# The first feed-forward of a fused block in six rounds of 4, 4, 4, 4, 4, 2 tiles in place of five of 6, 4, 4, 4, 4

## The chip, the cores and the metric

One core of one Trainium2 chip runs the kernel. The metric is device time in microseconds (us), the median of three runs. All times in the rows are microseconds from the start of one profiled execution.

## The reference, cut to what matters

The reference runs two layers of a mixed attention block, then a second block: a feed-forward with SwiGLU, a mixer of sparse and stick-breaking attention, a cross-attention to a memory of 256 tokens, and another feed-forward. There are 512 tokens (528 with the meta tokens of the first block) of width 1024; the inner width of the feed-forwards is 2816. What the change touches is this:

```
def swiglu(h, wg, wu, wd):
    return (jax.nn.silu(h @ wg) * (h @ wu)) @ wd
...
x = x + 0.5 * swiglu(rms_norm(x, ffn1_norm), ffn1_wg, ffn1_wu, ffn1_wd)
...
k = rms_norm((mem_n @ wk).reshape(B, M, MEM_HEADS, HEAD_DIM), g_k)     # in memory_cross_attention
v = (mem_n @ wv).reshape(B, M, MEM_HEADS, HEAD_DIM)
```

The memory's `k` and `v` depend on the input `mem` alone, so the kernel is free to place them early; it does so inside the first feed-forward.

## The kernel before

**Numbers.** Activations lie transposed, features on the 128 partitions and tokens along the free axis. Every fp32 operand of a large product is split into a high part (rounded to fp32r, by ScalarE) and a low part (the rest, by VectorE), and a product is three matmuls: high·high, high·low, low·high. `Stream` loads the weights in one fixed order (`weight_plan`) through SyncE's queue, and makes `whi` (line 135, ScalarE) and `wlo` (line 136, VectorE), each in three buffers, two entries ahead of use (`AHEAD = 2`).

**The feed-forward (`ffn`).** The inner width is 22 tiles of 128. They come in rounds (`ROUNDS`); `ffn_order` writes out the order. Within a round each tile is made by an "up" step, and after the round its tiles are multiplied by the down weights: eight `down` steps (one for each 128 of the 1024 outputs), each with 3 matmuls of 512 columns per tile of the round, and each ended by an addition into the residual `h` on VectorE (line 1266).

- Round 0 is *plain* (`up`): gate and up products over 8 blocks of the width, 2 × 8 × 3 = 48 matmuls of 512 columns per tile, then a scaling by the norm's factor, tanh, and products on VectorE.
- The later rounds are *blocks* (`up_blocks`): a 2×2 block scheme with seven products in place of eight, 7 × 4 × 3 = 84 matmuls of 256 columns per tile. It needs sums of weight blocks (`Stream.sums`, lines 156 to 159 and 164, 165, on VectorE and ScalarE), sums of activation blocks, and sums of the results (line 1188).
- Between the two stands *prepare*: it spreads the norm's factor (`Rn`), scales the residual (line 1160, 8 instructions), forms the activation sums `ta`, `tb` (lines 1167 to 1170) and splits them and the blocks `x0` to `x7` (lines 422 and 423). In the second feed-forward most of this is done earlier, during its plain tiles; in the first, where the memory's tensors occupy the space until their products are done, all of it comes after round 0.
- After prepare, `BEFORE[f]` of round 0's downs are emitted ahead of the first block tile; what is left of a round's downs is spread over the block tiles of the next round, and the last round's eight come at the end, each followed by the next norm's split and sum of squares (`norm_feed`).

The memory's products (`memory_kv`: first `k`, with a head norm on VectorE and a transpose, then `v`; 48 matmuls of 256 columns each) are put behind the plain tiles whose numbers `MEM_AT` gives.

**Order.** The kernel emits its instructions in this order, with some work put by an event queue that runs on an estimated clock (`at`, `soon`, `poll`); the framework (`schedule_with_timeline_sim=True`) then fixes one order per engine, by emission order and by the priorities raised with `high_priority`. Engines work in that order and wait for each other by semaphores. Three PSUM buffers (`mm`) take the plain and down products, two (`s`) share the block products.

Of the kernel before, what the change touches and what calls it, by code (L numbers as in the profile page):

```python
# [55 lines left out]
COLS = {"dq": 0, "dk": 512, "dv": 1024, "dg": 1536, "fq": 2048, "fk": 2560, "fv": 3072, "fg": 3592}  # L56
GA0 = (0, 2, 2, 0, 2, 0, 1, 1)
GA1 = (1, 1, 2, 0, 2, 0, 0, 2)
MEM_AT = (3, 5)

ROUNDS = {"ffn1": (6, 4, 4, 4, 4), "ffn2": (4, 4, 4, 4, 4, 2)}
EARLY, BLOCK_AHEAD = (7000.0, 11000.0), 3
BEFORE = {"ffn1": 8, "ffn2": 6}
ACTS = 8

S_LATE = 7
# [115 lines left out]
def ffn_order(f):  # L182


    out, m, down = [], 0, []
    for r, n in enumerate(ROUNDS[f]):
        for i in range(n):
            out.append(("blocks" if r else "plain", r, m + i, i))
            if f == "ffn1" and r == 0 and m + i in MEM_AT:
                out.append(("mem", r, m + i, i))  # L190
# [5 lines left out]
        if r == 0:  # L196
            out += [("prepare", r, 0, 0)] + down[:BEFORE[f]]
            down = down[BEFORE[f]:]
        m += n
# [3 lines left out]
def weight_plan(A):  # L203
# [16 lines left out]
    def halves(key, src, cols):  # L220
        for k in range(2):
            cut(key + (k,), src, cols, (512 * k, 512 * k + 512))

    def ffn(f):
        wg, wu, wd = (A[f"{f}_{x}_2"][0] for x in ("wg", "wu", "wd"))
        for kind, r, m, at in ffn_order(f):
# [6 lines left out]
            elif kind == "mem":  # L233
                x = "kv"[MEM_AT.index(m)]
                halves(("mem", x), A[f"mem_w{x}_2"][0], (0, 256))
# [61 lines left out]
class Net:  # L297
# [821 lines left out]
    def ffn(self, f, P, nxt, memory=None):  # L1119
# [4 lines left out]
        HT = T // 2  # L1124
        rounds = ROUNDS[f]
        with ExitStack() as st:
# [102 lines left out]
            for kind, r, m, at in ffn_order(f):  # L1229
# [11 lines left out]
                elif kind == "mem":  # L1241
                    mem("kv"[MEM_AT.index(m)])
                elif kind == "blocks":
# [870 lines left out]
```

## Time and profile before

| | us |
|---|---|
| median of 3 runs | 1791.04 (1790.66 to 1793.39) |
| the profiled execution: its own time | 1787.97 |
| the profiled execution: span from first to last instruction | 1786.2 |
| first feed-forward, first plain matmul to first matmul of the mixer | 672.1 to 1041.5 |
| second feed-forward | from about 1428 to the end |

PE is TensorE's matmuls, DVE VectorE, ACT ScalarE. A busy PE is one that always has a matmul under way. The granted clock (PEclk) is the share of full speed that TensorE was given; it has two levels, 1.2 and 2.4 GHz, and 1.00 is the higher. Matmul rows overlap: the pace is read from one start to the next.

### The profile page before, as it was taken

To read this page: it belongs to the slowest core of one execution; us is meant where nothing else is said; L and a number is where in the kernel's file an instruction comes from. 1 tells how busy PE (TensorE), PEld (TensorE's weight loads), DVE (VectorE), ACT (ScalarE), POOL (GpSimd) and SP (SyncE) were. 2 spreads that over 40 slices of the span, in tenths; PEclk is the share of its full clock that TensorE was granted. 3 is DMA by queue.
4 is the path that set the end of the run, shared out by engine and by line. 5 is a ranking of instruction groups with operands and counts; after the bars stand their busy time and mean duration, and the time that the engine had idled before them with its cause. 6 is when DMAs were issued, how large, how long until landed. Compare 5 with 4: busy or idle time off the path is not lost.

```text
span 1786.2 us, 31132 instructions
## 1 busy us (share of the span) xinstructions
PE 1723.6 (96%) x11949; PEld 1535.7 (86%) x11949; DVE 1384.1 (77%) x3305; ACT 940.9 (53%) x2051; POOL 33.6 (2%) x76
## 2 busy tenths in 40 slices
PE   7999999999999899999999999999978898999999
PEld 6999997998999678889999889877756787999997
DVE  6878666579876666699888778778787869988876
ACT  4656677356667863344433443457755634444432
POOL 1000000100000000000000000000000000000000
PEclk9999999999999999999999999999989999999999
DMA  4222211322222132332333243320101022333333
GB/s 159 74 69 72 67 54 37 95 60 83 70 74 60 37 120 83 109 128 83 101 105 109 70 142 129 91 71 14 37 24 48 31 76 95 96 100 102 100 91 104
DMA packets 56156, 146.00 MB, mean 82 GB/s; under 512 B 9032, under 2 KB 16840, under 8 KB 56008
## 3 DMA queue, kind: packets, MB, share of 16 engines
q1 hardware_dynamic: 54984, 143.95, 26.3%
q8 instruction: 94, 1.54, 0.3%
q14 instruction: 54, 0.44, 0.1%
q0 software_dynamic: 1024, 0.07, 0.1%
HBM read 141.83 MB, written 2.10 MB: 81 GB/s over the span
## 4 chain that ended last, share of the span: by engine, by line
PE 89%; DVE 6%; ACT 3%; issue 1%; DMA 1%; SPq 0%; ACTq 0%; DVEq 0%
PE mm L368 61%; PE s L368 18%; PE po L368 5%; PE pt L381 4%; PE pt L368 1%; DVE P L467 1%; DVE sc L1712 0%; DVE wlo L136 0%; ACT P L804 0%; ACT whi L135 0%; DMA w<-in_c_stream_dram 0%; DVE sbs L455 0%; ACT P L929 0%; DVE P L1714 0%; ACT PT L1616 0%
## 5 line engine op out<-in xcount | busy, mean ns | idle before, releaser
L135 ACT ACTIVATE whi<-w 128x1024 fp32r<-128x1024 f32 (+4 forms) x225 | 199.2, 886 | 267.0 <-PE mm L368 155.0
L136 DVE TENSOR_TENSOR wlo<-w,whi 128x1024 fp32r<-128x1024 f32 (+4 forms) x225 | 226.2, 1006 | 64.0 <-ACT whi L135 63.3
L368 PE MATMUL mm<-acth,whi 128*128 128x512 f32 x352 | 139.2, 397 | 3.5 <-DVE e L1143 1.7
L368 PE MATMUL mm<-actl,whi 128*128 128x512 f32 x352 | 139.7, 397 | 0.8 <-DVE actl L423 0.8
L368 PE MATMUL mm<-acth,wlo 128*128 128x512 f32 x352 | 139.3, 396 | 0.0
L381 PE MATMUL pt<-ident,P 128*128 128x128 f32 (+2 forms) x588 | 101.1, 282 | 17.6 <-DVE P L1714 11.7
L467 DVE CUSTOM_DVE_ANT_0 P<-s,mz 128x144 f32<-128x144 f32 (+8 forms) x195 | 82.8, 438 | 28.2 <-PE s L368 16.0
L381 PEld LDWEIGHTS pt<-ident,P 128*128 128x128 f32 (+2 forms) x588 | 65.2, 134 | 35.3 <-issue 15.7
L368 PE MATMUL mm<-cl,whi 128*128 128x264 f32 (+1 forms) x256 | 87.9, 344 | 0.5 <-DVE cl L1626 0.5
L368 PE MATMUL mm<-ch,wlo 128*128 128x264 f32 (+1 forms) x256 | 86.9, 341 | 0.5 <-DVE wlo L136 0.5
L368 PE MATMUL mm<-ch,whi 128*128 128x264 f32 (+1 forms) x256 | 84.7, 347 | 2.3 <-ACT ch L1008 1.4
L368 PEld LDWEIGHTS mm<-acth,whi 128*128 128x128 f32 x352 | 66.2, 188 | 19.3 <-DVE e L1143 2.1
L368 PEld LDWEIGHTS mm<-acth,wlo 128*128 128x128 f32 x352 | 66.3, 188 | 16.2 <-DVE wlo L136 0.2
L368 PEld LDWEIGHTS mm<-actl,whi 128*128 128x128 f32 x352 | 66.3, 188 | 15.8 <-DVE actl L423 1.3
L804 ACT ACTIVATE P<-P,nm 128x144 f32<-128x144 f32 (+4 forms) x136 | 68.0, 500 | 22.2 <-DVE nm L467 21.1
L1266 DVE SCALAR_TENSOR_TENSOR h<-mm,h 128x512 f32<-128x512 f32 x88 | 59.9, 682 | 9.7 <-PE mm L368 9.3
L164 ACT ACTIVATE whi<-sc 128x1024 fp32r<-128x1024 f32 x34 | 36.0, 1058 | 42.0 <-DVE sc L158 41.9
L368 PEld LDWEIGHTS mm<-ch,whi 128*128 128x128 f32 x256 | 47.2, 188 | 10.0 <-ACT ch L1008 2.3
L368 PE MATMUL s<-pk,pq 128*128 128x264 f32 (+4 forms) x171 | 54.4, 324 | 1.2 <-DVE nm L467 1.0
L368 PE MATMUL mm<-x0h,whi 128*128 128x264 f32 (+2 forms) x168 | 53.2, 317 | 1.5 <-DVE e L1143 0.6
L368 PE MATMUL mm<-x0h,wlo 128*128 128x264 f32 (+2 forms) x168 | 53.1, 316 | 0.9 <-DVE wlo L165 0.9
L368 PEld LDWEIGHTS mm<-ch,wlo 128*128 128x128 f32 x256 | 48.2, 188 | 6.4 <-DVE wlo L136 0.9
(840 smaller groups left out, 6032.8 us busy)
## 6 DMA issues: line engine op xcount, KB each, us to landing
w<-in_c_stream_dram SPq DMA_DIRECT2D x168, 512.0 KB, 3.6
w<-in_c_stream_dram SPq DMA_DIRECT2D x72, 256.0 KB, 2.6
w32b<-in_c_stream_dram SPq DMA_DIRECT2D x34, 512.0 KB, 3.6
w<-in_c_stream_dram SPq DMA_DIRECT2D x8, 384.0 KB, 3.1
h<-in_c_x_dram SPq DMA_DIRECT2D x8, 264.0 KB, 5.6
w1k<-in_cmp_w_k_dram SPq DMA_DIRECT2D x4, 512.0 KB, 5.4
w1v<-in_cmp_w_v_dram SPq DMA_DIRECT2D x4, 512.0 KB, 6.6
out_dram<-h SPq DMA_DIRECT2D x8, 256.0 KB, 2.0
```

Of the source, the lines that this page charges most:

```text
L135: nc.scalar.activation(out=hi, in_=w, func=AF.Copy)
L136: nc.vector.tensor_tensor(out=lo, in0=w, in1=hi.bitcast(F32), op=ALU.subtract)
L164: nc.scalar.activation(out=hi[:, :n], in_=src, func=AF.Copy)
L368: self.nc.tensor.matmul(out, lhsT, rhs, start=start, stop=stop)
L381: self.nc.tensor.transpose(out, in_, self.ident[:p, :p])
L467: self.nc.vector.tensor_tensor_reduce(out=dst, in0=s, in1=m, scale=-1.0, scalar=3.0e38, op0=ALU.add, op1=ALU.min, accum_out=nm)
L804: nc.scalar.activation(out=P_[:nq, a:b], in_=S[c][0], func=AF.Exp, bias=nm[:nq, 0:1], scale=S[c][1], accum_out=ls[:nq, c:c + 1])
L1266: v.scalar_tensor_tensor(out=H[m], in0=ps, scalar=0.25, in1=H[m], op0=ALU.mult, op1=ALU.add)
```

## The change

Three constants change: the first feed-forward's rounds, the plain tiles behind which the memory's products stand, and the number of round 0's downs that are emitted before the first block tile.

```diff
-MEM_AT = (3, 5)
-
-ROUNDS = {"ffn1": (6, 4, 4, 4, 4), "ffn2": (4, 4, 4, 4, 4, 2)}
+MEM_AT = (1, 3)
+
+ROUNDS = {"ffn1": (4, 4, 4, 4, 4, 2), "ffn2": (4, 4, 4, 4, 4, 2)}
 EARLY, BLOCK_AHEAD = (7000.0, 11000.0), 3
-BEFORE = {"ffn1": 8, "ffn2": 6}
+BEFORE = {"ffn1": 6, "ffn2": 6}
```

So two of the 22 tiles go from plain to blocks, there are six sets of eight downs in place of five (four tiles deep, the last two deep, where the first was six deep), `k` comes after plain tile 1 and `v` after plain tile 3, and two of round 0's downs go behind the first two block tiles. The order in which the weights are streamed follows.

## Rows read from the trace of the kernel before

**Rows 1.** The page's part 1: busy us, share, instructions.
```profile
PE 1723.6 (96%) x11949; PEld 1535.7 (86%) x11949; DVE 1384.1 (77%) x3305; ACT 940.9 (53%) x2051; POOL 33.6 (2%) x76
```
**Rows 2.** Timeline of PE: start, duration; pace of plain, memory and block tiles.
```profile
721.73 0.28 PE L368 MATMUL mm<-whi,x0h 128*128 128x256 f32 x1
...
727.33 0.39 PE L368 MATMUL mm<-x0h,whi 128*128 128x512 f32 x1
...
741.55 0.48 PE L368 MATMUL mm<-x4h,whi 128*128 128x512 f32 x1
...
749.93 0.28 PE L368 MATMUL mm<-whi,x0h 128*128 128x256 f32 x1
...
863.12 0.28 PE L368 MATMUL mm<-x0h,whi 128*128 128x256 f32 x1
...
873.12 0.40 PE L368 MATMUL mm<-acth,whi 128*128 128x512 f32 x1
```
**Rows 3.** Windows, first feed-forward: length, busy PE, PEld, DVE, ACT, POOL; PEclk, DMA.
```profile
756.50:790.20 33.70, 33.70 (x146) 27.09 (x146) 32.27 (x58) 15.30 (x26) 0.00 (x0) 1.00 0.39 129
756.50:773.35 16.85, 16.85 (x74) 13.54 (x74) 16.38 (x30) 8.38 (x16) 0.00 (x0) 1.00 0.45 156
857.50:873.12 15.62, 15.62 (x111) 14.52 (x109) 14.11 (x22) 6.35 (x9) 0.00 (x0) 1.00 0.39 119
1023.70:1045.80 22.10, 22.10 (x96) 17.78 (x95) 20.66 (x32) 15.69 (x24) 0.00 (x0) 1.00 0.50 144
```
**Rows 4.** Timeline of DVE: prepare's first instruction, the first block tile's last weight split.
```profile
757.85 0.74 DVE L1160 SCALAR_TENSOR_TENSOR yh<-h,gains,th 128x512 f32<-128x512 f32 x1
...
794.97 0.68 DVE L165 TENSOR_TENSOR wlo<-w32b,whi 128x512 fp32r<-128x512 f32 x1
```
**Rows 5.** Timeline of PE with the idle time before each: waits in both feed-forwards.
```profile
814.14 0.39 PE L368 MATMUL mm<-x0h,wlo 128*128 128x256 f32 x1 [0.69 <-DVE wlo L165]
...
824.54 0.39 PE L368 MATMUL mm<-x0h,whi 128*128 128x256 f32 x1 [0.32 <-ACT whi L164]
...
1476.98 0.50 PE L368 MATMUL mm<-acth,whi 128*128 128x512 f32 x1 [1.68 <-DVE e L1143]
...
1498.60 0.39 PE L368 MATMUL mm<-acth,whi 128*128 128x512 f32 x1
```
**Rows 6.** Groups of DVE by line and shape, 756.5 to 795.7: busy, mean ns.
```profile
L136 DVE TENSOR_TENSOR wlo<-w,whi 128x768 fp32r<-128x768 f32 x6 | 5.7, 947 | 0.8 <-ACT whi L135 0.8
L1266 DVE SCALAR_TENSOR_TENSOR h<-mm,h 128x512 f32<-128x512 f32 x8 | 5.4, 680 | 1.1 <-PE mm L368 1.1
...
L423 DVE TENSOR_TENSOR x2l<-yh,x2h 128x256 fp32r<-128x256 f32 x1 | 0.4, 415 | 0.0
```
**Rows 7.** The same groups of DVE, 850 to 912.4: four block tiles.
```profile
L136 DVE TENSOR_TENSOR wlo<-w,whi 128x512 fp32r<-128x512 f32 x8 | 5.5, 682 | 0.0
```
**Rows 8.** Windows of the second feed-forward: plain tiles 2 and 3, then downs.
```profile
1459.00:1473.00 14.00, 14.00 (x62) 11.43 (x61) 13.86 (x27) 6.97 (x13) 0.00 (x0) 1.00 0.20 57
1473.00:1495.40 22.40, 18.04 (x74) 13.25 (x73) 22.36 (x43) 10.55 (x18) 0.00 (x0) 1.00 0.20 59
```
**Rows 9.** Timeline of PE, ACT and DVE at the first feed-forward's plain tile 2.
```profile
699.62 0.39 PE L368 MATMUL mm<-x0h,whi 128*128 128x512 f32 x1
...
699.91 1.05 ACT L135 ACTIVATE whi<-w 128x1024 fp32r<-128x1024 f32 x1
700.42 2.73 DVE L668 SCALAR_TENSOR_TENSOR h<-h,gains,R 128x512 f32<-128x512 f32 x4
...
703.67 2.73 DVE L668 SCALAR_TENSOR_TENSOR h<-h,gains,R 128x512 f32<-128x512 f32 x4
...
706.92 1.22 DVE L136 TENSOR_TENSOR wlo<-w,whi 128x1024 fp32r<-128x1024 f32 x1
```
**Rows 10.** Timeline of PE in the memory stage: its longest wait there.
```profile
1398.09 0.58 PE L368 MATMUL s<-mk,mq 128*128 128x256 f32 x1 [4.63 <-ACT Pm L1981]
```
**Rows 11.** Window of the memory stage after that wait.
```profile
1398.00:1404.00 6.00, 5.91 (x31) 5.25 (x32) 5.69 (x21) 5.32 (x21) 0.00 (x0) 0.53 0.00 0
```

## The prediction

> **What bounds the kernel now.** I read the page first: PE is busy for 96% of the span [rows 1], so at first sight fewer matmuls mean less time. Then I followed the first feed-forward on PE's timeline, to see whether it paces the stage: from 672.1 to 1041.5 it waits twice, for 0.69 and 0.32 us, both times for the split of block weights by VectorE and ScalarE [rows 5]. So PE sets the pace, but VectorE is close behind. The windows show where: in the 33.70 us in which PE works off round 0's eight downs, VectorE is busy for 32.27 [rows 3]. It does prepare there, from 757.85 on, and ends the splits for the first block tile at 794.97 + 0.68 = 795.65 [rows 4], after PE has started that tile at 790.2. Round 0's downs, six tiles deep, are thus the cover for prepare, and a cover just long enough. Later there is more room: a block tile with two downs takes PE 15.62 us and VectorE 14.11 [rows 3].
>
> The second feed-forward already has the rounds that the first is to get. There VectorE is busy for 13.86 of 14.00 us and 22.36 of 22.40, and in the latter stretch PE works for 18.04 only [rows 8].
>
> **The change part by part.** The sum is made on the profiled execution's own 1787.97 us, which lies 3.07 below the median of the runs shown, 1791.04; I carry it over to the median. Less than 0.2% (3.6 us) can't be told from no change.
>
> *Two tiles from plain to blocks.* 36 plain matmuls take 749.93 − 741.55 = 8.38 us, 0.2328 each, so a plain tile's 48 take 11.17. A block tile's 84 take 873.12 − 863.12 = 10.00 [rows 2]. Twice the difference is **−2.3 us**. The down matmuls stay 22 × 3 × 8 = 528, and the memory's products stay as many as they are.
>
> *Eight more downs' endings and other weight loads.* Eight more additions into the residual cost VectorE 8 × 0.68 us [rows 6], and a block tile wants more of it than a plain one. In the rounds after the first block round this lies in the room of 15.62 − 14.11 = 1.5 us per tile [rows 3], and less is asked there of weights; I take nothing, and 1 us as the other bound. The stream's bytes are the same; the DMA engines are at 0.39 in the later block rounds [rows 3], so eight more loads cost nothing.
>
> *Prepare loses its cover.* It stands after `v` as before and can't start earlier: `Rn` is spread by PE only when `v`'s matmuls are issued, and the sums' space is the memory's. What VectorE has to do from there to the first block tile is 32.27 us less what shrinks: six weight splits of 768 columns at 0.95 become 512 wide at 0.68, −1.6 [rows 6, 7]; two downs, if they stay behind the block tiles, take with them 2 × 0.68 of addition and 2 × 0.68 of split, −2.7. That leaves 28.0 us. PE's cover is six downs of 12 matmuls, 16.85 us (a stretch of that length is in [rows 3]). The shortage is 11.1 us. If the framework brings the two downs forward, as it does in the second feed-forward, where down matmuls stand between a block tile's at 1498.60 [rows 5], the cover is 16.85 × 8/6 = 22.5, the work 30.7, and the shortage 8.2. If they stay, the two block tiles behind which they stand give some of the 11.1 back. The second feed-forward checks this from another side: its PE loses 22.40 − 18.04 = 4.4 us, though some 7.3 us of prepare are done there while plain tiles still run (of the 27 instructions 11 are for plain tiles and weights, and 13.86 − 11 × 0.6 is 7.3 [rows 8]), and six such instructions, 3.6 us, are left over into the downs. Without that lead, and with `v` as cover for the leftovers, 4.4 + 7.3 − 3.6 = 8.1. I take **+8.5 us**, with 4.4 and 11.1 as bounds. Behind VectorE, what stands still is PE alone; ScalarE is at 15.30 of 33.70 [rows 3].
>
> *The memory's `k` before plain tile 2.* Now tile 2 starts at 699.62 and its weights were ready before [rows 9]. With `k`'s weights ahead of them in the stream, two places of three buffers are taken, and tile 2's gate weights get the place that tile 3's have now: `whi` at 699.91, `wlo` at 706.92, because VectorE works off eight residual scalings first (line 668, 700.42 to 706.4), which were emitted earlier [rows 9]. `k` takes PE 727.33 − 721.73 = 5.6 us [rows 2], so tile 2 wants `wlo` with its third matmul, at about 699.6 + 5.6 + 0.5 = 705.7, and has it at 706.92 + 1.22 = 708.1. I take **+2.4 us**; bounds 0 (the framework puts this split ahead of the residual scalings) and 3.6 (it comes after one more instruction of its length). `k`'s head norm on VectorE comes in the plain tiles, where VectorE has room; the memory's split inputs are made while the layer before still runs, so they are not late. Queued behind the waiting matmul is all of PE; nothing else is near its limit there.
>
> *The last round is two deep.* Its eight downs have 6 matmuls each, 1.4 us at 0.234, while each asks VectorE for an addition, a split and a sum. In the 22.10 us from the first such addition to the last split VectorE is now busy for 20.66, three splits of the mixer's weights included [rows 3]. Five weight splits get narrower, 256 columns at 0.41 (the nearest row has that shape) for 0.68: 19.3 us are left. PE's own cover is seven downs, 9.8 us, and 4.9 us of the mixer's first product until that wants the last block of the width: 14.7. So PE waits 4.6 us, or nothing, if the framework fills in the mixer's second product up to the same point (another 4.9). I take **+2.0**.
>
> Sum: −2.3 + 8.5 + 2.4 + 2.0 = **+10.6 us**, 1798.6 on the profiled execution's scale and **1801.6** on the median's. With the lower bounds it is −2.3 + 4.4 = +2.1 (1793.1), with the upper ones −2.3 + 11.1 + 3.6 + 4.6 = +17.0 (1808).
>
> *A wait and the clock.* In the memory stage PE waits for 4.63 us in one piece, and in the 6 us from its next matmul on the granted clock is 0.53 on average, so mostly the lower level of 1.2 GHz [rows 10, 11]; 0.47 × 6 = 2.8 us of full-speed work are lost. In the second feed-forward's stretch the 4.4 us come in pieces of 1.68 at most [rows 5], and the clock stays at 1.00 [rows 8]. The Trainium skill, "TensorE: Matmul & The Clock Gate", section "HAM oscillation — how this bites in real kernels", says that long idle gaps of PE bring the half clock back, so that each gap is paid for again in the matmuls behind it. By that rule the 8.5 us, if they come in one piece, would cost more than themselves; both stretches of the trace agree with it.
>
> **The rivals.**
>
> *A: PE stays fed, and it gets faster.* Place: VectorE's order between `v` and the first block tile. If the framework puts what that tile's first products want ahead of the second tile's weight sums and of the additions, and the two downs are brought forward, the shortage could stay under the cushion that now lets VectorE end 5.5 us after the tile's start. For it: now PE loses nothing there. Against it: the second feed-forward, with the same rounds and a lead in prepare, does lose. Price: −2.3, and −1.0 more if the two waits of [rows 5] go as well: 1787.7 to 1788.7. It is faster than before as soon as all three waits together stay under 2.3 us, and measurably so only at its lower end.
>
> *B: PE loses what the second feed-forward loses, and no more.* `v` and the plain leftovers serve as the lead, the other two waits are hidden. For it: the same rounds, a measured 4.4. Against it: prepare has no start ahead of `v`. Price: +2.1, 1793.1, no change that can be told.
>
> *C: the wait for prepare comes in one piece, and the clock falls.* For it: [rows 10, 11]; against it: the second feed-forward's waits are cut up by downs whose PSUM buffers come free one by one. Price: 2.8 on top, 1804.4.
>
> **How the numbers follow.** My forecast has 0.62 (1794.6 to 1808), C 0.10, B 0.12, A 0.16, of which 0.09 is measurably faster. Slower by over 0.2%: 0.62 + 0.10 = 0.72; within 0.2%: 0.12 + 0.07 = 0.19; faster: 0.09. The range that holds 8 in 10 reaches from A's upper half, 1788.5, to the upper bounds' 1808; the forecast's own is 1794.6 to 1808.
>
> **What would show it.** Right: PE waits of 8 us in all between `v` and the end of the first block round, ended by VectorE (lines 165, 423 or 1160), VectorE over 95% busy there; a wait of some 2 us at plain tile 2 for `wlo`, line 136; waits of some 2 us between the last downs and the mixer's first products, ended by `h` (line 1266) or `x7l`; a plain tile at 11.2 and a block tile at 10.0 as before. Wrong: VectorE idle while PE waits, prepare starting before `v` ends, or PE without waits and a stage 2.3 us shorter.

## The result, and the profile after

The kernel with the change takes 1804.42 us in the median (1801.68 to 1805.61) against 1791.36 for the kernel before on the same chip (1790.66 to 1793.39): a ratio of 1.0073, with a 95% interval of 1.0059 to 1.0086. It is slower by 13.1 us (10.6 to 15.4), where 10.6 were forecast. The profiled execution took 1804.56 us by its own time, with a span of 1802.8, and that is what the rows below show.

The page's part 1 of the kernel after, to be read against [rows 1]:

```profile
PE 1732.2 (96%) x12021; PEld 1544.0 (86%) x12021; DVE 1399.2 (78%) x3339; ACT 946.7 (53%) x2065; POOL 33.6 (2%) x76
```

This view hides the loss: PE has less work and is busy for 8.6 us more, still 96% of a longer span. The loss is in the waits, and in a lower granted clock behind some of them. The timeline of PE of the kernel after, with the idle time before each matmul, from the first plain tile to the mixer:

```profile
710.84 0.75 PE L368 MATMUL mm<-x0h,wlo 128*128 128x512 f32 x1 [1.87 <-DVE wlo L136]
...
758.83 0.39 PE L368 MATMUL mm<-x4h,whi 128*128 128x256 f32 x1 [0.62 <-DVE h L1266]
...
761.17 0.38 PE L368 MATMUL mm<-x0h,wlo 128*128 128x256 f32 x1 [1.83 <-DVE wlo L165]
...
769.79 0.39 PE L368 MATMUL s<-x4h,wlo 128*128 128x256 f32 x1 [0.90 <-DVE wlo L165]
...
778.49 0.39 PE L368 MATMUL mm<-x4h,whi 128*128 128x256 f32 x1 [0.35 <-DVE s L1188]
...
803.77 0.36 PE L368 MATMUL s<-ta0h,whi 128*128 128x256 f32 x1 [0.53 <-DVE e L1188]
...
1051.88 0.50 PE L368 MATMUL mm<-acth,wlo 128*128 128x512 f32 x1 [0.87 <-DVE wlo L136]
...
1053.86 0.50 PE L368 MATMUL mm<-x0h,whi 128*128 128x512 f32 x1 [0.78 <-ACT whi L135]
...
1055.55 0.71 PE L368 MATMUL mm<-x0h,wlo 128*128 128x512 f32 x1 [0.96 <-DVE wlo L136]
...
1073.47 1.16 PE L368 MATMUL pt<-ident,rt 128*128 128x128 f32 x8 [0.87 <-DVE nm__17338 L495]
```

Where [rows 5] had two waits in the first feed-forward, 1.01 us together, there are now three groups: one wait at plain tile 2 (1.87), five around the first block round (4.23 together), three at the seam to the mixer (2.61). All but one of these nine are ended by VectorE. It also ends a wait of 0.87 behind the seam, before the mixer's first transposes. The windows of the kernel after at these places (length; busy PE, PEld, DVE, ACT, POOL; granted clock; DMA), as in [rows 3]:

```profile
707.00:716.00 9.00, 7.13 (x29) 5.58 (x29) 8.27 (x15) 2.75 (x4) 0.00 (x0) 0.81 0.39 106
739.80:757.90 18.10, 18.10 (x83) 14.35 (x82) 17.08 (x34) 9.68 (x18) 0.00 (x0) 1.00 0.42 146
739.80:813.90 74.10, 69.87 (x467) 63.45 (x466) 72.50 (x123) 35.43 (x55) 0.00 (x0) 0.98 0.35 110
...
1048.00:1052.00 4.00, 3.13 (x14) 2.19 (x13) 4.00 (x9) 3.14 (x6) 0.00 (x0) 1.00 0.55 159
1052.00:1056.00 4.00, 2.26 (x7) 1.27 (x8) 4.00 (x6) 2.41 (x4) 0.00 (x0) 0.96 0.53 173
1056.00:1060.00 4.00, 4.00 (x13) 3.13 (x12) 3.79 (x8) 2.06 (x3) 0.00 (x0) 0.62 0.71 211
```

VectorE is busy for 72.50 of the 74.10 us after `v`, and for all of 1048 to 1056, in which PE works for 5.39 of 8.00. The clock falls below 1.00 at each of the three places (0.81 at tile 2, 0.98 after `v`, 0.96 and 0.62 at the seam), while in [rows 3] it stands at 1.00 throughout.

**A ledger of the stage.** Four starts of PE cut it up: the transposes of the norm's factor, ahead of plain tile 2; the first down; the last block matmul; the mixer's first transposes. The timeline of PE of the kernel before, with one matmul of the mixer behind the last start, then of the kernel after, whose fourth start is 1073.47 above:

```profile
696.91 1.95 PE L368 MATMUL pt<-ident,nr 128*128 128x128 f32 x16
...
756.34 0.48 PE L368 MATMUL mm<-acth,whi 128*128 128x512 f32 x1
...
1013.32 0.28 PE L368 MATMUL s<-tb3h,wlo 128*128 128x256 f32 x1
...
1056.56 1.05 PE L368 MATMUL pt<-ident,rt 128*128 128x128 f32 x8
...
1057.78 0.39 PE L368 MATMUL mm<-whi,x6h 128*128 128x256 f32 x1
```
```profile
699.56 1.95 PE L368 MATMUL pt<-ident,nr 128*128 128x128 f32 x16
...
740.59 0.48 PE L368 MATMUL mm<-acth,whi 128*128 128x512 f32 x1
...
1029.18 0.28 PE L368 MATMUL s<-tb3h,wlo 128*128 128x256 f32 x1
```

That the first start is 2.65 later in the kernel after comes from ahead of the change and isn't counted: from 600 to 620 the granted clock was 0.74 there and 0.91 before. With plain tiles at 11.17 us [rows 2], downs at (863.12 − 857.50) / 24 = 0.2342 a matmul [rows 2, 3], and block tiles at the pace of before, (256.98 − 408 × 0.2342) / 16 = 10.09, the loss of each part beyond its work is:

- plain tiles and memory: 41.03 − (59.43 − 2 × 11.17) = **+3.9**
- blocks: 288.59 − (18 × 10.09 + 432 × 0.2342) = **+5.8**
- end of the stage: 44.29 − (43.24 − 24 × 0.2342) = **+6.7**
- two tiles from plain to blocks: 2 × (10.09 − 11.17) = **−2.2**

The sum is +14.3 in the profiled execution, beside the timed 13.1. Of the end's 6.7, 0.7 are no loss but order. In the kernel before, the transposes come ahead of `x6` and `x7` of a mixer product (1057.78 above), in the kernel after behind them, and these are six matmuls of 0.119 [rows 2]. So the end loses 6.0 and the stage some 13.5. The same 0.7 lies in every end of the table below (0.5 in run 1). Its reference is one execution of the kernel before, 3.4 us below that kernel's median, with the clock at 1.00 in the whole stage.

### The profile page after: what moved, and what is told of

It reads as the page before. It is cut to its first block, busy times and chain, and to the rows that moved or that the text cites. A ratio compares the mean times of both kernels' runs of the same rounds, so it can differ in the third digit from the quotient of the medians.

```text
span 1802.8 us, 31361 instructions
## 1 busy us (share of the span) xinstructions
PE 1732.2 (96%) x12021; PEld 1544.0 (86%) x12021; DVE 1399.2 (78%) x3339; ACT 946.7 (53%) x2065; POOL 33.6 (2%) x76
## 3 DMA queue, kind: packets, MB, share of 16 engines
q1 hardware_dynamic: 56136, 143.95, 25.8%
## 4 chain that ended last, share of the span: by engine, by line
PE 83%; DVE 11%; ACT 3%; issue 1%; DMA 1%; POOL 0%; SPq 0%; DVEq 0%; ACTq 0%
PE mm L368 56%; PE s L368 17%; PE po L368 5%; PE pt L381 4%; DVE wlo L136 1%; PE pt L368 1%; DVE P L467 1%; DMA w<-in_c_stream_dram 1%; DVE h L1266 1%; DVE wlo L165 1%; DVE sc L1712 1%; DVE sbs L455 0%; ACT P L804 0%; DVE h L668 0%; DVE P L1714 0%
## 5 line engine op out<-in xcount | busy, mean ns | idle before, releaser
L135 ACT ACTIVATE whi<-w 128x1024 fp32r<-128x1024 f32 (+3 forms) x229 | 196.6, 859 | 268.7 <-PE mm L368 141.7
L136 DVE TENSOR_TENSOR wlo<-w,whi 128x1024 fp32r<-128x1024 f32 (+3 forms) x229 | 222.7, 973 | 69.6 <-ACT whi L135 69.0
L381 PEld LDWEIGHTS pt<-ident,P 128*128 128x128 f32 (+2 forms) x588 | 66.2, 136 | 35.6 <-issue 15.9
L1266 DVE SCALAR_TENSOR_TENSOR h<-mm,h 128x512 f32<-128x512 f32 x96 | 65.4, 683 | 9.1 <-PE mm L368 9.1
```

Source lines behind the costliest of these rows:

```text
L135: nc.scalar.activation(out=hi, in_=w, func=AF.Copy)
L136: nc.vector.tensor_tensor(out=lo, in0=w, in1=hi.bitcast(F32), op=ALU.subtract)
L381: self.nc.tensor.transpose(out, in_, self.ident[:p, :p])
L1266: v.scalar_tensor_tensor(out=H[m], in0=ps, scalar=0.25, in1=H[m], op0=ALU.mult, op1=ALU.add)
```

## The experiments

Each ran beside the kernel before on the same chip. The table gives the timed difference, (ratio − 1) × 1791 with its interval, and the ledger of its profiled execution, worked out in the same way with the tiles and downs of its own rounds; "work" is the ledger's last item.

| run | timed, us | plain | blocks | end | work | ledger's sum |
|---|---|---|---|---|---|---|
| the change | +13.1 (10.6 to 15.4) | +3.9 | +5.8 | +6.7 | −2.2 | +14.3 |
| 1 before, memory early | +3.2 (1.3 to 5.2) | +2.2 | −0.1 | +0.5 | 0 | +2.5 |
| 2 change, `k` after tile 2 | +11.3 (8.8 to 13.8) | +0.2 | +5.9 | +7.2 | −2.2 | +11.2 |
| 3 change, last round 4 deep | +8.6 (5.7 to 11.5) | +4.0 | +6.9 | +1.1 | −2.2 | +9.8 |
| 4 change, all downs first | +15.0 (12.4 to 17.7) | +4.0 | +7.5 | +6.6 | −2.2 | +15.9 |
| 5 change, sums ahead of tile 3 | +26.1 (23.5 to 28.8) | | | +7.0 | −2.2 | +28.3 |
| 6 change, lows on GpSimd | +16.8 (14.3 to 19.3) | +4.0 | +8.3 | +6.6 | −2.2 | +16.6 |
| 7 run 5, last round 4 deep | +23.8 (21.3 to 26.3) | | | +1.4 | −2.2 | +25.0 |
| 8 before, last round 2 deep | +9.8 (7.5 to 12.4) | 0.0 | +3.4 | +5.8 | 0 | +9.2 |
| 9 change, one pair of sums | +6.3 (4.1 to 8.6) | +2.4 | +0.9 | +7.1 | −2.2 | +8.3 |
| 10 half of the change | +1.1 (−0.5 to 2.9) | +0.1 | +4.1 | +0.8 | −1.1 | +3.9 |
| 11 all three cured | +1.1 (−0.5 to 2.7) | +0.2 | +3.1 | +1.5 | −2.2 | +2.7 |

In runs 5 and 7 downs come ahead of the last plain tile, so the first two parts can't be told apart there; together they give +23.4 and +25.8.

**1. The memory's products early, alone.** On the kernel before:

```diff
-MEM_AT = (3, 5)
+MEM_AT = (1, 3)
```

> The kernel before, with the memory's products behind plain tiles 1 and 3 and nothing else of the change. Theory (each part of the change costs at its own place): plain tile 2 waits about 1.9 us for its low weights (line 136), and the clock is halved for some 3.4 us after it, as in the changed kernel; 2 to 4 us slower than before, 1793.5 to 1795.5. Rival (all that was lost comes from the rounds, the memory's products can stand anywhere): no wait at tile 2, the time of before, 1791.4 within 1 us.

It took 1792.87 us (1789.43 to 1798.02), ratio 1.0018 (1.0007 to 1.0029). The wait at plain tile 2 is there, as long as in the kernel after, but the clock holds. The timeline of PE, then the window of the same length as the first one above, of this run:

```profile
707.53 0.50 PE L368 MATMUL mm<-x0h,wlo 128*128 128x512 f32 x1 [1.87 <-DVE wlo L136]
```
```profile
707.00:716.00 9.00, 8.46 (x37) 6.92 (x38) 8.38 (x20) 3.36 (x5) 0.00 (x0) 1.00 0.55 161
```

So the early `k` costs by itself, in the plain tiles and nowhere else, since the 0.5 in this run's end is the order of the mixer's matmuls. Its 3.2 us by the ratio are measurably more than the rival's nothing, and by the median less than the theory's.

**2. `k` behind plain tile 2.** On the kernel after:

```diff
-MEM_AT = (1, 3)
+MEM_AT = (2, 3)
```

> The changed kernel with the memory's k behind plain tile 2 in place of 1 (v stays behind tile 3). Theory: the weights of tile 2 have the places in the buffers that they had before, the wait of 1.87 us and the half clock after it go, 3 to 4 us faster than the changed kernel, 1800.5 to 1801.5. Rival: the wait only moves to the next tile or to the memory's products, and the time stays at 1804.4 within 1 us.

1802.51 us (1799.52 to 1803.3), ratio 1.0063 (1.0049 to 1.0077). No wait is left at tile 2, and the loss of the plain part falls from 3.9 to 0.2. The timed ratios give 1.8 us with intervals that overlap, so the time alone doesn't show it; the theory's range was missed by 1.

**3. The last round four deep.** On the kernel after, the short round goes one place forward:

```diff
-ROUNDS = {"ffn1": (4, 4, 4, 4, 4, 2), ...
+ROUNDS = {"ffn1": (4, 4, 4, 4, 2, 4), ...
```

> The changed kernel with rounds of 4, 4, 4, 4, 2, 4, so that the last eight downs are four deep again. Theory (VectorE can't follow downs of 1.4 us each, and the next norm and the mixer's first weights come late): the waits of 0.87, 0.78, 0.96 and 0.87 us at the end of the stage and the half clock between them go, 5 to 6 us faster than the changed kernel, 1798.5 to 1799.5. Rival (the loss is prepare's lost cover and nothing else): 1804.4 within 1 us.

1798.99 us (1795.82 to 1802.49), ratio 1.0048 (1.0032 to 1.0064), as the theory had it. The end's loss falls from 6.7 to 1.1; the short round costs less where it is now. Its one new wait, on the timeline of PE of this run:

```profile
1000.86 0.47 PE L368 MATMUL mm<-acth,whi 128*128 128x512 f32 x1 [0.77 <-DVE s L1188]
```

**4. All of round 0's downs ahead of the blocks.** On the kernel after:

```diff
-BEFORE = {"ffn1": 6, "ffn2": 6}
+BEFORE = {"ffn1": 8, "ffn2": 6}
```

> The changed kernel with all eight downs of round 0 emitted ahead of the first block tile (8 in place of 6). Theory (the framework brings the two downs forward anyway, VectorE is what is short): within 1 us of the changed kernel's 1804.4, the same 4 us of waits in the first block round. Rival (the two downs behind the block tiles are the cover that is missing): the waits shrink by the two downs' 5.6 us to nothing, some 4 us faster, 1800.4.

1805.86 us (1801.49 to 1808.38), ratio 1.0084 (1.0069 to 1.0099). The theory's bound was passed by 0.5. Where the two downs stand isn't what costs: with both emitted first, nothing is won.

**5. Prepare's sums ahead of the last plain tile.** On the kernel after, both memory products come behind plain tile 2 (`MEM_AT = (2, 2)`), and behind them, ahead of plain tile 3:

```diff
+                elif kind == "sums":
+                    self.wait(lambda: "k" in self.mem_done)
...
+                    ys = [tiles_of() for _ in range(4)]
+                    for j in range(4):
+                        scaled(j, Rn, self.g_ffn1, ys[j])
+                        sums(j, ys[j])
```

> The changed kernel, with both memory products behind plain tile 2 and with prepare's eight scalings and sixteen activation sums emitted right behind them, ahead of plain tile 3 (four pairs of scaled tiles in place of two); only the splits of the blocks x0 to x7 stay after the plain tiles. Theory (prepare lost its cover, and VectorE needs a lead): the wait at plain tile 2 goes (2 us, as in the run with k after plain tile 2), and of the 6 to 8 us around the first block tile at least half goes, since one plain tile's 11 us take in part of prepare: 1796.5 to 1800. Rival (the first block tile waits for its weight sums and not for prepare): only tile 2's wait goes, 1802 to 1803; the waits for wlo of line 165 stay at 1.8 and 0.9.

1815.97 us (1813.88 to 1820.79), ratio 1.0146 (1.0131 to 1.0161): both were wrong. The timeline of DVE, then of PE, of this run:

```profile
737.23 0.75 DVE L1161 SCALAR_TENSOR_TENSOR yh<-h,gains,th 128x512 f32<-128x512 f32 x1 [0.81 <-ACT th L512]
...
756.31 0.69 DVE L424 TENSOR_TENSOR tb3l<-e,tb3h 128x512 fp32r<-128x512 f32 x1
756.91 0.69 DVE L1144 TENSOR_TENSOR e<-mm,R 128x512 f32<-128x512 f32 x1
```
```profile
757.66 0.79 PE L369 MATMUL mm<-acth,whi 128*128 128x512 f32 x1 [21.08 <-DVE e L1144]
```

Prepare didn't get a lead. It still began only at 737.23, when tile 3's matmuls were done, and then ran for 19.7 us, with one gap of 0.36, ahead of tile 3's evictions (line 1144, which is 1143 in the kernel after). The next downs needed tile 3, and PE stood still. So the run says nothing for either side on amounts; it gives prepare's length on VectorE, 19.7 us for its 40 instructions, and shows that the order on that engine can cost more than the amount.

**6. The low parts of the sums on GpSimd.** On the kernel after, the eight subtractions of `ta` and `tb`:

```diff
-                    B[x, j] = self.split(self.parts_of(tp, f"t{x}{j}", T), src)
+                    hi, lo = B[x, j] = self.parts_of(tp, f"t{x}{j}", T)
+                    nc.scalar.activation(out=hi, in_=src, func=AF.Copy)
+                    (nc.gpsimd if f == "ffn1" else v).tensor_tensor(out=lo, in0=src, in1=hi.bitcast(F32), op=ALU.subtract)
```

> The changed kernel, with the eight subtractions that make the low parts of the activation sums ta and tb (128 x 512 each, 0.68 us on VectorE) moved from VectorE to GpSimd in the first feed-forward. Theory (VectorE's work is what is late at the first block tile): VectorE has 5.4 us less to do there, and PE's waits between v and the second block round shrink by 3 to 5 us: 1799.5 to 1801.5. Rival (the order, or the two engines' common use of SBUF, not the amount of work): no change or slower, 1804 to 1806.

1807.33 us (1806.31 to 1808.22), ratio 1.0094 (1.008 to 1.0108). The rival held, by its second half, with a time 1.3 us above its range. The timelines of POOL and of DVE of this run:

```profile
765.20 7.71 POOL L1174 TENSOR_TENSOR ta2l<-e,ta2h 128x512 fp32r<-128x512 f32 x1 [4.36 <-ACT ta2h L1173]
772.87 2.27 POOL L1174 TENSOR_TENSOR ta3l<-e,ta3h 128x512 fp32r<-128x512 f32 x1
...
776.80 1.73 POOL L1174 TENSOR_TENSOR tb3l<-e,tb3h 128x512 fp32r<-128x512 f32 x1
```
```profile
775.61 1.78 DVE L156 TENSOR_TENSOR sb<-w32b 128x512 f32<-128x512 f32 x1
777.31 1.78 DVE L159 TENSOR_TENSOR sb<-w,w32b 128x512 f32<-128x512 f32 x1
779.01 0.68 DVE L157 TENSOR_TENSOR sc<-sb,w 128x512 f32<-128x512 f32 x1
```

While GpSimd subtracts, the weight sums on VectorE take 1.78 us; after its last instruction, at 778.53, they take 0.68 again, and GpSimd's own subtraction is once shown as 7.71 long. The two engines hinder each other, and VectorE is no less late. The Trainium skill ("SBUF — State Buffer", section "SBUF: two separate sides") says that VectorE with two inputs from SBUF and GpSimd share one pair of ports, which one instruction holds to its end; the rows agree.

**7. Run 5 with the last round four deep.**

> The kernel of e5 with rounds of 4, 4, 4, 4, 2, 4, so that neither tile 2's wait, nor the late prepare, nor the two-deep last round is left. Theory (the three losses add up and are independent): e5's time less 5.4, so 1791 to 1794.5, and 1789 if early sums take away all of prepare's loss. Rival (the losses are one lag that is passed on, and what is cured in one place comes back in the next): 1795 or more.

1814.13 us (1811.7 to 1817.29), ratio 1.0133 (1.0119 to 1.0147). It inherits run 5's 21 us wait, so the bounds of both sides are void. The end's loss falls from 7.0 to 1.4 as in run 3, and 2.4 of that are lost again in the parts before, where the short round now stands; the timed difference to run 5 is 2.3 us.

**8. A short last round on the kernel before.**

```diff
-ROUNDS = {"ffn1": (6, 4, 4, 4, 4), ...
+ROUNDS = {"ffn1": (6, 4, 2, 4, 4, 2), ...
```

> The kernel before with rounds of 6, 4, 2, 4, 4, 2 in place of 6, 4, 4, 4, 4: the last round two deep and one more round, and nothing else. Theory (a two-deep last round costs by itself, since each of its eight short downs asks VectorE for as much as a long one): 5 to 6 us slower than the kernel before, 1796 to 1797.5, with waits at the end of the stage for wlo and whi, lines 136 and 135. Rival (the tail loses only because VectorE comes into it late from prepare): 1791 to 1792.5.

1800.7 us (1799.52 to 1801.31), ratio 1.0055 (1.0042 to 1.0069). The rival is refuted: nothing is late from prepare here, and the end loses all the same (5.8 in the table, some 5 without the 0.7), by the same three waits. The timeline of PE of this run:

```profile
1045.84 0.50 PE L368 MATMUL mm<-acth,wlo 128*128 128x512 f32 x1 [0.87 <-DVE wlo L136]
...
1047.72 0.50 PE L368 MATMUL mm<-x0h,whi 128*128 128x512 f32 x1 [0.69 <-ACT whi L135]
...
1049.50 0.59 PE L368 MATMUL mm<-x0h,wlo 128*128 128x512 f32 x1 [1.04 <-DVE wlo L136]
```

The total is above the theory's, since the two-deep round in the middle and the sixth round cost 3.4 more.

**9. One pair of activation sums.** On the kernel after:

```diff
             def sums(j, tiles):
+                if f == "ffn1" and j:
+                    B["a", j], B["b", j] = B["a", 0], B["b", 0]
+                    return
```

> The changed kernel, with the activation sums ta and tb of the first feed-forward formed and split for the first of the four pairs of blocks only and used for all four: it leaves out 12 sums and 6 splits on VectorE, 12 x 0.34 + 6 x 0.60 = 7.7 us by their pace, and nothing else of the work. Theory (in prepare VectorE is what is late, by 6 to 8 us): the waits between v and the second block round shrink by 5 to 7 us, 1797 to 1799.5. Rival (the order of the first block tile, or its weight sums, is late whatever prepare does, as the runs with the sums earlier and on GpSimd could be read): under 2 us less, 1802.5 or more.

1796.62 us (1793.99 to 1799.05), ratio 1.0035 (1.0023 to 1.0048): 7.8 us less than the change by the medians, 6.8 by the ratios, at the theory's upper end and beyond. The run leaves out three of the four pairs' sums, so it is no version to use. With 7.7 us less for VectorE in prepare, of the five waits around the first block round the longest is left, 0.22 of the first, and a new one of 0.18. The timeline of PE, then the window from `v` to the second block round, of this run:

```profile
756.29 0.39 PE L368 MATMUL mm<-x0h,wlo 128*128 128x256 f32 x1 [1.83 <-DVE wlo L165]
```
```profile
735.60:804.80 69.20, 66.97 (x467) 61.94 (x466) 64.94 (x105) 32.34 (x49) 0.00 (x0) 1.00 0.37 117
```

The same 467 matmuls take 69.20 us in place of 74.10, at a clock of 1.00 in place of 0.98, with VectorE at 94% in place of 98%. The 1.83 us belong to the block weights' own split and stay, so the rival is right for that one wait only. Six roundings of ScalarE (line 422, 0.63 us each) go with the sums; that ScalarE was not the limit is argued from its 35.43 busy us of 74.10, and from the four waits that shrank or went, all ended by VectorE.

**10. Half of the change.** On the kernel after:

```diff
-MEM_AT = (1, 3)
+MEM_AT = (2, 4)
...
-ROUNDS = {"ffn1": (4, 4, 4, 4, 4, 2), ...
+ROUNDS = {"ffn1": (5, 4, 3, 3, 3, 4), ...
...
-BEFORE = {"ffn1": 6, "ffn2": 6}
+BEFORE = {"ffn1": 8, "ffn2": 6}
```

> Half of the change and no short last round: rounds of 5, 4, 3, 3, 3, 4 tiles, the memory's products behind plain tiles 2 and 4, all eight of the first downs ahead of the blocks. One tile fewer is plain (1.2 us less work on TensorE). Theory (the cover of the first downs is then 8 x 15 matmuls, 28 us, for 30 to 31 us of VectorE's work, and the three-deep rounds and the sixth round cost 1 to 2 us): 1791 to 1794.5. Rival (with the cover almost whole and neither tile 2's wait nor a two-deep last round, what is left is the saving): 1789.5 to 1790.5, which would beat both kernels.

1792.04 us (1788.66 to 1794.28), ratio 1.0006 (0.9997 to 1.0016): level with the kernel before, in the theory's range. A cover of 28 us is nearly enough; two longer waits are left where it ends, with a granted clock of 0.66 from 780 to 785. The timeline of PE of this run:

```profile
778.52 0.36 PE L368 MATMUL mm<-x0h,whi 128*128 128x256 f32 x1 [1.15 <-DVE h L1266]
...
779.87 0.39 PE L368 MATMUL s<-ta0h,whi 128*128 128x256 f32 x1 [0.88 <-ACT whi L164]
```

**11. All three losses treated**: run 9 with `MEM_AT = (2, 3)` and rounds of 4, 4, 4, 4, 2, 4.

> The changed kernel with all three losses treated: k behind plain tile 2, rounds of 4, 4, 4, 4, 2, 4, and the activation sums formed for one pair of blocks only (12 sums and 6 splits on VectorE left out). Theory (three separate losses that add up): the run with one pair of sums, less 2 for k and less 5.4 for the last round: 1789.5 to 1792.5, the kernel before within its own scatter. Rival (one lag that moves on): 1794 or more.

1791.14 us (1790.1 to 1794.23), ratio 1.0006 (0.9997 to 1.0015), so 12.0 of the 13.1 us are gone. One by one the cures gave 1.8 (run 2), 4.5 (run 3) and 6.8 (run 9), 13.1 together: within the intervals they add up, and no lag moved on from one place to the next. The two longer waits that remain, on the timeline of PE of this run, are the weights' split of run 9, this time with a granted clock of 0.67 from 753.8 to 759, and the short round in the middle:

```profile
753.82 0.39 PE L368 MATMUL mm<-x0h,wlo 128*128 128x256 f32 x1 [1.84 <-DVE wlo L165]
...
992.87 0.47 PE L368 MATMUL mm<-acth,whi 128*128 128x512 f32 x1 [0.84 <-DVE s L1191]
```

No version beat the kernel before. Even the run that leaves work out of prepare doesn't show the 2.2 us that the blocks save.

## Why the prediction was right, and where its terms were off

It was right in sign and, nearly, in size, for the reasons given: VectorE can't prepare the blocks, feed the plain tiles and end the downs under less cover. The terms were off in both directions and made up for each other, so that the sum came so close is in part luck.

- **Two tiles from plain to blocks, −2.3.** Right. A block tile of the kernel after starts at 857.81 and the down behind it at 867.80, 9.99 us, as [rows 2] had it, on the timeline of PE:

```profile
857.81 0.28 PE L368 MATMUL mm<-x0h,whi 128*128 128x256 f32 x1
...
867.80 0.40 PE L368 MATMUL mm<-acth,whi 128*128 128x512 f32 x1
```

- **Eight more downs' endings, nothing.** Right within its bound of 1: run 9 loses 0.9 in all of the blocks, its wait of 1.83 included.
- **Prepare loses its cover, +8.5: the cause was right, the size too large.** That it is VectorE's work is shown by run 9. It cost 5.8 in the profiled execution: the five waits (4.23), and some 0.02 × 74.1 = 1.5 of half clock. The step that failed is "That leaves 28.0 us. PE's cover is six downs": it asked for all of prepare to be done when the first block tile starts. The timeline of DVE of the kernel after shows sums for later products formed 18 us after that tile's start at 757.8:

```profile
762.29 0.69 DVE L423 TENSOR_TENSOR tb1l<-e,tb1h 128x512 fp32r<-128x512 f32 x1
...
776.21 0.69 DVE L423 TENSOR_TENSOR tb3l<-e,tb3h 128x512 fp32r<-128x512 f32 x1
```

  The first block products need `x` and the block weights alone, so the tile covers part of prepare itself: 16 of prepare's 40 instructions on VectorE start after it, some 7.5 of the 19.7 us of run 5. The prediction had seen this as a cushion of 5.5 us under rival A and left it out of the sum. That prepare would begin when `v` ends was right: 741.62 after 739.8. The two downs came forward in part: their first matmuls stand within the first two block tiles, at 763.77 and 780.11.
- **`k` before plain tile 2, +2.4.** Right, step by step. `wlo` was put at 706.92; it came at 709.56 in an execution that is 2.65 later at that point, behind the residual scalings as said. The timeline of DVE of the kernel after:

```profile
706.31 2.73 DVE L668 SCALAR_TENSOR_TENSOR h<-h,gains,R 128x512 f32<-128x512 f32 x4
708.96 0.68 DVE L1146 SCALAR_TENSOR_TENSOR e<-th,e 128x512 f32<-128x512 f32 x1
709.56 1.22 DVE L136 TENSOR_TENSOR wlo<-w,whi 128x1024 fp32r<-128x1024 f32 x1
```

  The loss is 2.2 and 2.4 where the clock holds (runs 1 and 9), and 3.9 where it falls, as in the kernel after.
- **The two-deep last round, +2.0: too small, beyond its bound of 4.6.** It loses 6.0 (6.7 in the table), and some 5 on the kernel before (run 8), and a four-deep last round takes 5.6 of it away in the ledger, 4.5 of the timed difference (run 3). The step that failed is the cover of 14.7 us, of which 4.9 were the mixer's first product "until that wants the last block of the width". PE never got to that point: it waits for the last down's `wlo`, then for `whi` and `wlo` of the mixer's first weights, while VectorE is busy for 8.00 of 8.00 us. These weights were late from the start: `whi` had to wait for their transfer, and SP's queue, which issues it, for a buffer that VectorE's split of other weights gives free. The timeline of ACT and SP's waits (total, times, longest) from 1030 to 1060 of the kernel after:

```profile
1052.74 1.06 ACT L135 ACTIVATE whi<-w 128x1024 fp32r<-128x1024 f32 x1 [1.05 <-DMA w<-in_c_stream_dram]
```
```profile
SPq L143 <- DVE wlo L136: 14.0, 9, 2.9
```

  In the kernel before SP waits for such buffers as well, 17.0 us in 8 waits from 1014 to 1044, so this line doesn't show a cause of its own. No run takes work from VectorE at this place alone, so how much is its own order and how much the transfers stays open. A product whose own weights pass through the engine that is short of time is no cover for that engine. About 1.4 of the 6.0 are half clock: seven matmuls from 1056.05 on stand 0.43 apart in place of 0.23.
- **Rival A** (faster): refuted, and run 11 shows that with nearly all losses cured it would be level. **Rival B** (only 4.4 lost, the rest hidden): its 4.4 is about what prepare's waits came to, 4.23, but the other two losses were not hidden. **Rival C** (the wait in one piece, and the clock falls): the wait came in five pieces, and yet the clock fell, here and at two other places, for some 1.5 + 1.5 + 1.4 = 4.4 us in the profiled execution. The forecast's sum had no term for that. Without it and the 0.7 of order the ledger stands at some 9, near the forecast's 10.6. That C's price, 1804.4, is the measured time is luck: its one long wait didn't come.

## What to carry to other kernels

Where PE is busy for 96%, count for each stretch what the second engine must do in it: a change that takes work from PE may take the cover from that engine, and a shallow last round, with as many endings under half the matmuls, can lose more than its saving. Before counting a product as cover, ask which engine makes its operands. Price waits of a few us with what the clock may take behind them, and check whether the losses add up by curing each alone and all together.

## What the runs showed of the hardware

The same wait at plain tile 2, 1.87 us to the hundredth, stands in six of the profiled executions. In four (the kernel after and runs 3, 4 and 6) the matmuls behind it were 0.43 us apart for seven or eight in a row, the lower clock; in two (runs 1 and 9) they kept 0.23 and the window's clock is 1.00. At the seam to the mixer the clock fell in five of seven executions with a short last round. In the second feed-forward waits of some 1.7, 0.8 and 1.6 us follow each other in every traced execution; the kernel before kept 1.00 there [rows 8], which the prediction took as a row against rival C, but in six of the thirteen traces the clock fell behind them (0.91 from 1479 to 1499 in run 1). So the length of a wait doesn't settle whether the clock falls, and what does stays open here. With a fall behind the wait at tile 2 the plain part lost 3.9 to 4.0 us, without one 2.2 to 2.4. The Trainium skill ("TensorE: Matmul & The Clock Gate", section "HAM oscillation — how this bites in real kernels") has long gaps bring the half clock back; these runs show that gaps far below the 4.63 us of [rows 10] can do so, and that they need not.
